# Matmul, bias and tanh on one core: twelve loads of the third column's leaving pair moved from GpSimd's DMA queue to SyncE's

## The chip, the cores and the metric

The kernel runs on one core of a Trainium2 chip. The core has a TensorE (PE in the profile; PEld is its weight load), a VectorE (DVE), a ScalarE (ACT), a GpSimd (POOL) and a SyncE (SP). Transfers between the chip's memory (DRAM) and the core's on-chip memory run on 16 DMA engines, and an instruction on POOL, SP or ACT issues them. The profile names two queues that matter here: q0, to which POOL's issues go ("software_dynamic"), and q1, to which SP's go ("hardware_dynamic"). The metric is device microseconds of one execution, the median of several.

## The reference

```python
m, k, n = 4096, 4096, 4096          # a: m x k, b: k x n, bias: n, all float32
return np.tanh(np.matmul(a, b) + bias)
```

## The kernel before

The output is made in four columns of 1024 (c = 0 to 3), and in each column in 16 row pairs of 256 rows. One row pair of one column is a 2 x 2 of 128 x 512 tiles, and the kernel makes it with seven products instead of eight, in the manner of Strassen and Winograd. `a` and `b` are split into quarters a11..a22 and b11..b22 (float16); the products are m2 = s2 b11, m5 = s5 b22, m3 = a11 d3, m1 = s1 d1, m4 = a22 d4, m6 = s6 e6 and m7 = s7 e7. s2, s5, s1, s6 and s7 are sums of quarters of `a`; d3 = b12 + b22, d1 = b11 - b22, d4 = b11 + b21, e6 = b11 + b12 and e7 = b21 + b22 belong to the column. Each right-hand operand is four blocks of 128 x 4 x 512 (`b11_0` to `b11_3` and so on); blocks 0 of b11 and of e6 are the two halves of a tile named `side`. A product of one row pair is 16 matmuls of 128 x 512.

From the second column on, row pairs are taken two at a time and some products are split once more in the same manner. In the third and fourth columns all seven are, in the function `four(n)`. For this the operands of m2 and m6 are cut into forms in DRAM (`form_m`), which are streamed through the on-chip places of b11 and e6; so b11 and e6 themselves are gone while this lasts. Some blocks of d3, d4, e7 and b22 are overwritten by a sum called t3, after their own contents have been put into DRAM (`away_m_t`).

The last two row pairs of a column are taken as a duo that shares operands with the next column: first both with blocks 0 and 1 of every operand (part 0), then both with blocks 2 and 3 (part 1), then the same two row pairs for the next column. They need b11, e6 and the rest whole. So the pair ahead of the duo in the third column leaves the split form: in `four` the flag `leave` is true for it alone, its products m1, m6 and m7 are done whole (`whole`, L961), and `give_back(c, step)`, called at numbered steps of `four` and, for steps from 18 on, from slots of the duo, brings the operands back. The table `BACK` says at which step which of them comes: ("b11", 2) is block 2 of b11; ("m5", "t3") is what t3 has overwritten in b22, ("m7", "t3") in e7, ("m3", "t3") in d3 and ("m4", "t3") in d4; ("b12", 0) and ("b21", 0) are raw blocks of the next column, which later sums need. A block of b11 or e6 that is not in `BACK` comes as soon as its place has been read for the last time (`let_go`). A block of b11 comes in two halves of 128 x 4 x 256 (256 KB each), one from `form_m` and one from `form_m` or `corner`; a raw block comes in one piece of 512 KB from a float16 copy (`cast`).

Instructions run in the order in which the program issues them, on each engine and each queue. What the leaving pair does on SP: it stores outputs (L493, from tiles `o`, `s`, `ds`), gives back the t3 places (L644) and fetches the quarters of `a` of the coming duo (L312, from `scratch`, 256 KB for each row pair of the duo). The output tiles `o` come from a pool of three, so a new one waits for the store of the one three back. In the leaving pair's tail DVE writes `o` for the second row pair (`take_m5(q)`), and behind that it takes m1 of the first row pair out of its bank into `s` (`take_m1(p)`); PE adds m7 of the first row pair into the same bank after that.

```python
        if leave:
            take_m5(q)
            take_m1(p)
```

Of the kernel before, what the change touches and what calls it, by code (L numbers as in the profile page):

```python
# [13 lines left out]
TB = 4  # L14
# [78 lines left out]


BACK = {
# [3 lines left out]
}  # L99

PLACE = {
# [6 lines left out]
HALF = (ds(0, NB // 2), ds(NB // 2, NB // 2))  # L108
# [14 lines left out]
def kernel(  # L123
# [7 lines left out]
    nc = tc.nc  # L131
# [218 lines left out]
    bop, raw = {}, {}  # L350
# [4 lines left out]
    def new_bop(name, blk):  # L355
        if blk == 0 and name in ("b11", "e6"):
            bop[name, blk] = side[:, :, ds(0 if name == "b11" else NB, NB)]
        else:
            bop[name, blk] = bops.tile([P, TB, NB], fp16, name=f"{name}_{blk}", tag=f"{name}_{blk}")
        return bop[name, blk]  # L360
# [3 lines left out]
    def cast_b(c, blk, h, j):  # L364
        cast[c, blk, h, j] = dram.tile([P, TB, NB], fp16, name=f"cast_{c}_{blk}_{h}_{j}")
        load_b(cast[c, blk, h, j], c, blk, h, j)

    def load_b(dst, c, blk, h, j, nt=TB):
        there = cast.get((c, blk, h, j))
        if there is not None and there is not dst:  # L370
            nc.gpsimd.dma_start(out=dst, in_=there)
            return
        off = b.offset + (2 * blk + h) * TB * QP * N + c * NCW + j * NB
        dx, dt = (1, QP) if h or blk else (TB, 1)
        for t in range(0, TB, nt):
            for q in (0, 2, 1, 3):
                src = bass.AP(
                    tensor=b.tensor, offset=off + (q * KQ + t * dt) * N,
                    ap=[[dx * N, QP], [dt * N, nt], [1, NB]],
                )  # L380
                nc.gpsimd.dma_start(out=dst[ds(q * QP, QP), ds(t, nt)], in_=src)  # L381

    def load_raw(name, c, blk):
        raw[name, blk] = wide.tile([P, TB, NB], fp16, name=name, tag="wide")
        nt = TB // 2 if c == 2 and name == "b21" else TB
        load_b(raw[name, blk], c, blk, *((0, 1) if name == "b12" else (1, 0)), nt)

    def load_op(name, c, blk):
        load_b(new_bop(name, blk), c, blk, *((0, 0) if name == "b11" else (1, 1)))
# [244 lines left out]
    def move(what, c, out_, *names):  # L634

        for name, (r, j) in (OVER_FOUR if c in FOURS else OVER).items():
            if names and name not in names:
                continue
            if out_:
                away[what, c, name] = dram.tile([P, TP, NB // 2], fp16, name=f"away_{what}_{c}_{name}")  # L640
            for i in range(2):
                there = away[what, c, name][:, ds(i * TB, TB)]
                here = quarter(what, r, j, i)
                nc.sync.dma_start(*(there, here) if out_ else (here, there))  # L644
# [94 lines left out]
    forms, blocks, queue, pulled = {}, {}, [], [0]  # L739
# [70 lines left out]
        corners[name, blk] = dram.tile([P, TB, NB // 2], fp16, name=f"corner_{name}_{blk}")  # L810
        nc.gpsimd.dma_start(out=corners[name, blk], in_=bop[name, blk][:, :, HALF[1]])

    def bring_block(c, name, blk):
        if (c, name, blk) not in blocks:
            what = {"b11": "m2", "e6": "m6"}[name]
            r, i = divmod(blk, 2)
            to = new_bop(name, blk)
            for j in range(2):
                there = corners[name, blk] if (r, j) == (0, 1) else forms[what, (r, j)][:, ds(i * TB, TB)]
                nc.gpsimd.dma_start(out=to[:, :, HALF[j]], in_=there)  # L820
            return
        nc.gpsimd.dma_start(out=new_bop(name, blk), in_=blocks[c, name, blk])

# [11 lines left out]
    def let_go(what, name):  # L835
        tag = held.pop((what, name))
        if returned and not queue and tag != "sum":
            name, blk = tag[:-2], int(tag[-1])
            if (name, blk) not in BACK:
                bring_block(returned[0], name, blk)  # L840
        else:
            free.append(tag)
        pull_four()
# [141 lines left out]
    def give_back(c, step):  # L985
        for (name, part), at in BACK.items():
            if at == step:
                if name in ("m3", "m4", "m5", "m7"):
                    move(name, c, False, part)
                elif name in ("b12", "b21"):  # L990
                    load_raw(name, c + 1, part)
                else:
                    bring_block(c, name, part)

    left_over = []

    def four(n):
# [11 lines left out]
        def step(k):  # L1009
            if leave:  # L1010
                give_back(c, k)
# [152 lines left out]
        if leave:  # L1164
# [27 lines left out]
            for k in range(18, 29):  # L1192
                at_slot(SLOTS * m + k - 18, give_back, c, k)
# [293 lines left out]
    def change(c, part, n):  # L1487


        s0 = SLOTS * n  # L1490
        blks = (2 * part, 2 * part + 1)
        for i, blk in enumerate(blks):
            at_slot(s0 + 1, load_op, "b11", c, blk)
            at_slot(s0 + 3, load_op, "b22", c, blk)
            at_slot(s0 + (4 if part else -3), load_raw, "b12", c, blk)
            at_slot(s0 + (8 if part else -2), load_raw, "b21", c, blk)
            s1 = s0 + 2 * part + i
            at_slot(s1 + 8, bsum, "d3", blk)
            at_slot(s1 + 9, bsum, "e6", blk)
            at_slot(s1 + 11, bsum, "d1", blk)  # L1500
            at_slot(s1 + 12, bsum, "d4", blk)
            at_slot(s1 + 13, bsum, "e7", blk)
# [87 lines left out]
    def load_first(m, queue, out_):  # L1590
# [9 lines left out]
        out=ident, in_=ident, compare_op=mybir.AluOpType.is_equal, fill=0.0,  # L1600
# [146 lines left out]
    for c in TWICE:  # L1747
# [24 lines left out]
        if c in STREAMED:  # L1772
            later = 8
            for at, name in zip((15, 15, 15, 16, 17, 19, 20), STREAM):
                at_slot(s0 + at, put_form, c, name)
            for blk in range(4):
                at_slot(s0 + 21, put_block, c, "e6", blk)
                at_slot(SLOTS * streams[c][-1] + 15, bring_block, c, "e6", blk)
            at_slot(s0 + 30, begin, c)
# [60 lines left out]
    for slot in range(1 - len(ORDER), SLOTS * len(items)):  # L1840
        if slot in handed:
            if slot - 1 not in handed:
                c = max(c for c in FOURS if SLOTS * (begins[c] - 2) < slot)
# [50 lines left out]
```

## Time and profile before

| | |
|---|---|
| median of 3 runs | 1524.16 us (1523.2 to 1524.38) |
| profiled execution | 1524.36 us, span 1522.6 us |
| TensorE busy | 1507.8 us, 99% of the span |
| DVE, ACT, POOL busy | 78%, 25%, 33% |
| q0 (POOL) / q1 (SP) | 203.22 MB / 185.24 MB |

The profiled execution lies 0.2 us above the median, and 1.8 us of it lie outside the span. The leaving pair of the third column stands at about 1060 to 1114 us from the span's start, the duo's part 0 in the third column at about 1114 to 1138 (its m6 and m7 end a little later, among products of part 1). The rows of the profile that matter for the change stand in the prediction. In the views of the profile, a row's "x" is a count; in the view of a DMA queue in a window the columns are packets, MB, and the time of its packets as a share of 16 engines.

### The profile page before, as it was taken

Reading aid. Unit: us, or ns where it says so; the run is one execution under the profiler, and the core shown is the slowest. Engines: PE = TensorE matmul, PEld = TensorE weight load, DVE = VectorE, ACT = ScalarE, POOL = GpSimd, SP = SyncE. Lnnn points to the kernel's source line nnn. Section 1 sums busy time; section 2 is a strip of 40 time slices with the busy share of each in tenths; the row PEclk is TensorE's granted clock in tenths of the full one; section 3 lists DMA queues with packets and bytes.
Section 4 is the critical chain, followed back from the end, with each engine's and each line's share of the span. In section 5 each row is a group of like instructions: output and inputs, shape, how many; then the busy total and the mean of one; then the engine's idle time right before and its main releaser. Section 6 shows DMA issues by size and latency. Waiting matters only on the chain.

```text
span 1522.6 us, 24007 instructions
## 1 busy us (share of the span) xinstructions
PE 1507.8 (99%) x9101; PEld 890.3 (58%) x9101; DVE 1182.2 (78%) x1644; ACT 380.1 (25%) x830; POOL 497.0 (33%) x893
## 2 busy tenths in 40 slices
PE   9999999999999999999999999999799999999999
PEld 4444444444445666544444578888544458888887
DVE  6789877777876666677787788888648869888888
ACT  4431111111221122111122223333113222333332
POOL 8775443333513231333543311111313121111112
PEclk9999999999999999999999999999899999999999
DMA  9999999999979998999998978889876687888895
GB/s 186 186 209 254 267 254 213 216 213 236 188 219 298 255 286 262 233 254 232 238 189 253 291 279 306 305 322 334 280 257 211 217 259 267 314 306 312 319 342 191
DMA packets 207672, 390.39 MB, mean 256 GB/s; under 512 B 25538, under 2 KB 103874, under 8 KB 207556
## 3 DMA queue, kind: packets, MB, share of 16 engines
q0 software_dynamic: 119616, 203.22, 57.5%
q1 hardware_dynamic: 87268, 185.24, 34.9%
q8 instruction: 71, 1.16, 0.3%
q10 hardware_dynamic: 672, 0.39, 0.1%
q14 instruction: 45, 0.37, 0.1%
HBM read 337.65 MB, written 136.84 MB: 312 GB/s over the span
## 4 chain that ended last, share of the span: by engine, by line
PE 97%; DMA 2%; DVE 0%; POOL 0%; ACT 0%; issue 0%; POOLq 0%; ACTq 0%; DVEq 0%
PE ps L478 55%; PE ps L897 27%; PE ps L1523 5%; PE ps L961 5%; PE ps L678 4%; DMA out_dram<-o 2%; DMA side<-in_b_dram 0%; DVE ps L153 0%; POOL first L1592 0%; POOL side L1612 0%; DVE a L153 0%; DVE ds L153 0%; ACT o L502 0%; DVE h L153 0%; DVE s L153 0%
## 5 line engine op out<-in xcount | busy, mean ns | idle before, releaser
L478 PEld LDWEIGHTS <-a 128*128 128x128 f16 x3136 | 306.9, 98 | 364.5 <-issue 0.4
L478 PE MATMUL ps<-b,a 128*128 128x512 f16 x1092 | 249.2, 379 | 0.0
L897 PEld LDWEIGHTS <-h 128*128 128x128 f16 x2176 | 212.7, 98 | 27.0 <-DVE h L153 0.8
L833 POOL DMA_DIRECT2D form<-form_m x147 | 77.7, 529 | 412.3 <-PE ps L897 370.0
L478 PE MATMUL ps<-d,a 128*128 128x512 f16 x896 | 202.5, 379 | 0.0
L478 PE MATMUL ps<-e,a 128*128 128x512 f16 x876 | 199.4, 379 | 0.0
L278 DVE STREAM_TRANSPOSE a<-nat 128x1024 f16<-128x1024 f16 (+2 forms) x202 | 175.2, 911 | 19.1 <-PE ps L478 17.6
L897 PEld LDWEIGHTS <-a 128*128 128x128 f16 x1632 | 159.6, 98 | 25.3 <-issue 0.9
L478 PE MATMUL ps<-d,s 128*128 128x512 f16 x624 | 141.0, 379 | 0.0
L250 POOL DMA_DIRECT2D nat<-in_a_dram x176 | 92.9, 533 | 133.8 <-DVE a L278 67.2
L478 PEld LDWEIGHTS <-s 128*128 128x128 f16 x816 | 79.8, 98 | 94.1
L381 POOL DMA_DIRECT2D b<-in_b_dram x192 | 103.4, 545 | 82.1 <-DVE a L278 31.0
L153 DVE TENSOR_TENSOR a<-a,a 128x2048 f16<-128x2048 f16 (+1 forms) x103 | 123.7, 1201 | 0.2
L897 PE MATMUL ps<-form,h 128*128 128x256 f16 x848 | 108.1, 273 | 0.0
L153 DVE TENSOR_TENSOR h<-a,h 128x1024 f16<-128x1024 f16 x136 | 92.4, 686 | 12.8 <-PE ps L897 12.7
L502 ACT ACTIVATE o<-ps 128x512 f32<-128x512 f32 x88 | 52.9, 601 | 153.0 <-issue 101.8
L897 PE MATMUL ps<-form,a 128*128 128x256 f16 x672 | 83.7, 273 | 0.1
L961 PE MATMUL ps<-d,a 128*128 128x512 f16 x352 | 79.4, 379 | 0.0
L153 DVE TENSOR_TENSOR ds<-ds,ps 128x512 f32<-128x512 f32 (+1 forms) x101 | 66.8, 672 | 12.6 <-PE ps L961 7.0
L983 ACT CAST ps<-zeros 128x256 f32<-128x256 f16 x140 | 50.1, 380 | 96.2 <-DVE s L153 51.3
L961 PEld LDWEIGHTS <-a 128*128 128x128 f16 x416 | 41.1, 99 | 55.0 <-issue 11.6
L153 DVE TENSOR_TENSOR ps<-ps,x 128x256 f32<-128x256 f32 x88 | 37.8, 429 | 41.8 <-PE ps L897 26.6
(198 smaller groups left out, 1967.4 us busy)
## 6 DMA issues: line engine op xcount, KB each, us to landing
form<-form_m POOLq DMA_DIRECT2D x147, 512.0 KB, 7.0
a<-scratch SPq DMA_DIRECT2D x140, 512.0 KB, 7.2
out_dram<-o SPq DMA_DIRECT2D x199, 256.0 KB, 5.7
nat<-in_a_dram POOLq DMA_DIRECT2D x288, 128.0 KB, 6.4
scratch<-a SPq DMA_DIRECT2D x48, 512.0 KB, 6.5
b<-in_b_dram POOLq DMA_DIRECT2D x160, 128.0 KB, 5.4
scratch<-a SPq DMA_DIRECT2D x32, 256.0 KB, 6.2
cast<-in_b_dram POOLq DMA_DIRECT2D x64, 128.0 KB, 9.6
```

The costliest lines, as they stand in the source:

```text
L153: nc.vector.tensor_tensor(out=out_, in0=in0, in1=in1, op=op)
L250: nc.gpsimd.dma_start(out=tl[ds(q * QP, QP), :, :], in_=src.rearrange("(mb p) k -> p mb k", p=QP),)
L278: nc.vector.transpose(dst[:, ds(b0 * tb, n * tb), :].rearrange("P (b t) (mb p) -> P mb b t p", t=tb, p=QP), src[:, :, ds(b0, n), :].rearra ...
L381: nc.gpsimd.dma_start(out=dst[ds(q * QP, QP), ds(t, nt)], in_=src)
L478: nc.tensor.matmul(st[where], at, bt, start=(what == "m2" or n < LEAD and what == "m1") and i == 0, stop=i == len(ts_) - 1, skip_group_che ...
L502: nc.scalar.activation(o, src, TANH)
L678: nc.tensor.matmul(to, at, bt, start=False, stop=t == TP - 1, skip_group_check=True)
L833: nc.gpsimd.dma_start(out=rights[what, name], in_=forms[what, name])
L897: nc.tensor.matmul(to, at, bt, start=False, stop=t == TP - 1, skip_group_check=True)
L961: nc.tensor.matmul(to[:, half], at[:, t // TB, t % TB], bop[right, t // TB][:, t % TB, half], start=anew and t == 0, stop=t == T - 1, skip ...
L983: nc.scalar.copy(bank(n, 0, where)[:, HALF[half]], zeros)
L1523: nc.tensor.matmul(mb[m % 4, j], aq[m, kt // T][:, kt % T, :], right(kt, j), start=fresh and kt == k0, stop=stop and kt == k1 - 1, skip_gr ...
```

## The change

Three things change. `BACK` is a new table: blocks 0 and 1 of b11 now come at steps 9 and 10 (before, block 0 at step 9, and block 1 as soon as its place was free), blocks 2 and 3 at step 17 (before 10 and 11), b22's t3 places at step 11 (before 10), those of d4 and d3 at 15 and 16 (before 17 and 16), the next column's b12 blocks at 18 (before 17), its b21 blocks at 19 as before. `load_raw`, `load_b` and `bring_block` take a queue, and `give_back` hands them SP's for the b12 and b21 blocks, and for every b11 or e6 block from step 8 on; that is b11 alone, since e6 blocks 0 and 1 are at 6 and 7 and blocks 2 and 3 come through `let_go`. PE, DVE and ACT execute the same instructions in the same order as before.

```diff
 BACK = {
-    ("m4", "t3"): 17, ("m3", "t3"): 16, ("m7", "t3"): 8,
-    ("b12", 0): 17, ("b12", 1): 17, ("b21", 0): 19, ("b21", 1): 19,
-    ("b11", 0): 9, ("e6", 0): 6, ("e6", 1): 7, ("m5", "t3"): 10, ("b11", 2): 10, ("b11", 3): 11,
+    ("e6", 0): 6, ("e6", 1): 7, ("m7", "t3"): 8, ("m5", "t3"): 11, ("b11", 0): 9, ("b11", 1): 10,
+    ("m3", "t3"): 16, ("b11", 2): 17, ("b11", 3): 17, ("m4", "t3"): 15,
+    ("b12", 0): 18, ("b12", 1): 18, ("b21", 0): 19, ("b21", 1): 19,
 }
+DIRECT = 8
...
-    def load_b(dst, c, blk, h, j, nt=TB):
+    def load_b(dst, c, blk, h, j, nt=TB, queue=nc.gpsimd):
...
-            nc.gpsimd.dma_start(out=dst, in_=there)
+            queue.dma_start(out=dst, in_=there)
...
-    def load_raw(name, c, blk):
+    def load_raw(name, c, blk, queue=nc.gpsimd):
...
-    def bring_block(c, name, blk):
+    def bring_block(c, name, blk, queue=nc.gpsimd):
...
-                nc.gpsimd.dma_start(out=to[:, :, HALF[j]], in_=there)
+                queue.dma_start(out=to[:, :, HALF[j]], in_=there)
...
                 elif name in ("b12", "b21"):
-                    load_raw(name, c + 1, part)
+                    load_raw(name, c + 1, part, nc.sync)
                 else:
-                    bring_block(c, name, part)
+                    bring_block(c, name, part, nc.gpsimd if step < DIRECT else nc.sync)
```

On SP, from the return of e7's t3 places (`e_0`, `e_1`) to the fourth store of the stage, there stood before (`b_0`, `b_1` are b22's places, `out_dram<-o` the stores):

```order
L644 DMA e_0_6535<-away_m_2_t_6891 128x4x256
L644 DMA e_1_6567<-away_m_2_t_6891 128x4x256
L493 DMA out_dram<-o 128x512 x3
L644 DMA b_0_6261<-away_m_2_t_6569 128x4x256
L644 DMA b_1_6266<-away_m_2_t_6569 128x4x256
L493 DMA out_dram<-o 128x512
```

and now, with line numbers one higher (`side` is b11 block 0, `b_1_9925` is block 1):

```order
L645 DMA e_0_6535<-away_m_2_t_6891 128x4x256
L645 DMA e_1_6567<-away_m_2_t_6891 128x4x256
L821 DMA side<-form_m_0_6764 128x4x256
L821 DMA side<-corner_b_0_6889 128x4x256
L494 DMA out_dram<-o 128x512 x3
L821 DMA b_1_9925<-form_m_0_6764 128x4x256
L821 DMA b_1_9925<-corner_b_1_6927 128x4x256
L494 DMA out_dram<-o 128x512
```

Two halves of a b11 block stand ahead of the three stores now and two behind them.

Further along on SP, at the end of the leaving pair, there stood before, between its last stores and the next column's bias (`d_0_6513`, `d_1_6537` are d4's places; `a_10069`, `a_10072` and `a_10128` are a21, a11 and a12 of the duo's part 1):

```order
L493 DMA out_dram<-ds 128x512
L644 DMA d_0_6513<-away_m_2_t_6856 128x4x256
L644 DMA d_1_6537<-away_m_2_t_6856 128x4x256
L312 DMA a_10069<-scratch_107 128x1024
L312 DMA a_10069<-scratch_106 128x1024
L312 DMA a_10072<-scratch_107 128x1024
L312 DMA a_10072<-scratch_106 128x1024
L312 DMA a_10128<-scratch_107 128x1024
L312 DMA a_10128<-scratch_106 128x1024
L405 DMA bias_bc<-in_bias_dram 128x512 x2
```

and now, from the second half of b11's block 2 on (`a_10065` and `a_10068` are a21 and a11, `a_10128` is a12 still; the four `b` from `cast` are the next column's b12 and b21):

```order
L821 DMA b_2_10059<-form_m_5_6886 128x4x256
L821 DMA b_3_10062<-form_m_2_6827 128x4x256
L821 DMA b_3_10062<-form_m_5_6886 128x4x256
L313 DMA a_10065<-scratch_107 128x1024
L313 DMA a_10065<-scratch_106 128x1024
L313 DMA a_10068<-scratch_107 128x1024
L313 DMA a_10068<-scratch_106 128x1024
L372 DMA b_10071<-cast_0_0_1_3504 128x2048
L372 DMA b_10073<-cast_1_0_1_3585 128x2048
L372 DMA b_10100<-cast_0_1_0_3874 128x2048
L372 DMA b_10102<-cast_1_1_0_3988 128x2048
L313 DMA a_10128<-scratch_107 128x1024
```

Four halves of b11 now stand ahead of a21 of part 1, and four blocks of 512 KB ahead of its a12. POOL's queue lost twelve rows: the eight halves of b11 and the four raw blocks; behind e6's eight halves it now has the next column's b11 and b22 at once.

More of the change, by code (lines that the diff above doesn't have):

```diff
@@ L381, in load_b @@
                 nc.gpsimd.dma_start(out=dst[ds(q * QP, QP), ds(t, nt)], in_=src)
-    def load_raw(name, c, blk):
+    def load_raw(name, c, blk, queue=nc.gpsimd):
         raw[name, blk] = wide.tile([P, TB, NB], fp16, name=name, tag="wide")
         nt = TB // 2 if c == 2 and name == "b21" else TB
-        load_b(raw[name, blk], c, blk, *((0, 1) if name == "b12" else (1, 0)), nt)
+        load_b(raw[name, blk], c, blk, *((0, 1) if name == "b12" else (1, 0)), nt, queue)
     def load_op(name, c, blk):
```

## The prediction

> **What bounds the kernel now.** I read the page first, then the waits of TensorE, the chain that ended last, the timeline around the one long wait, and then the DMA queues in short windows.
>
> ```profile
> PE 1507.8 (99%) x9101; PEld 890.3 (58%) x9101; DVE 1182.2 (78%) x1644; ACT 380.1 (25%) x830; POOL 497.0 (33%) x893
> ...
> PE ps L961 <- DVE s L153: 8.8, 1, 8.8
> PE warm L1583 <- DVE idle L416: 1.3, 1, 1.3
> ```
>
> TensorE is busy for 99% of the span, and of its waits (columns: total us, times, longest) one is long: 8.8 us at L961, the whole products of the leaving pair. The next is 1.3 us at the start. The change can therefore win this one wait and what hangs on it, or open new ones. The chain (start us, us, what) tells what it waited for:
>
> ```profile
> 1082.41 17.66 DMA out_dram<-o
> 1100.07 0.02 issue
> 1100.09 0.04 DVE o L153
> 1100.13 0.57 issue
> 1100.70 0.69 DVE s L153
> 1101.38 0.04 issue
> 1101.43 12.26 PE ps L961 x48
> 1113.68 100.15 PE ps L478 x464
> ...
> 1369.03 3.45 PE ps L961 x16
> ```
>
> The first of three stores needed 17.66 us to land. DVE's `take_m5(q)` needed its tile, `take_m1(p)` stood behind that on DVE, and TensorE restarted 1.36 us after the landing (1101.43 less 1100.07). The 48 matmuls behind it took 12.26 us, where 16 such take 3.45, so 10.35 at full speed. The timeline gives when TensorE was ready, and windows give the granted clock:
>
> ```profile
> 1089.84 2.75 PE L961 MATMUL ps<-e,a 128*128 128x512 f16 x12
> ...
> 1092.60:1101.40 8.80, 0.00 (x0) 0.10 (x1) 1.31 (x3) 0.54 (x1) 0.00 (x0) 0.62 0.88 315
> 1101.40:1105.20 3.80, 3.77 (x10) 1.42 (x10) 1.17 (x2) 0.72 (x2) 0.00 (x0) 0.53 0.71 212
> 1105.20:1113.50 8.30, 8.30 (x40) 3.69 (x39) 1.37 (x2) 1.26 (x2) 0.00 (x0) 1.00 0.87 285
> ```
>
> TensorE had ended at 1092.59, waited to 1101.43, and then had a clock of 0.53 for 3.8 us (third last column) before it was at 1.00 again. The stall costs 8.84 of waiting and 1.9 of slow clock, 10.7 us together; that is the most this stage can give.
>
> Why a store of 256 KB takes 17.66 us is in the queues (packets, MB, share; then issues with the us to landing):
>
> ```profile
> q0 software_dynamic: 585, 1.91, 66.3%
> q1 hardware_dynamic: 620, 1.05, 35.3%
> ...
> e<-away_m_t SPq DMA_DIRECT2D x2, 256.0 KB, 18.5
> e<-form_m POOLq DMA_DIRECT2D x1, 256.0 KB, 9.7
> ...
> q0 software_dynamic: 153, 0.50, 86.2%
> q1 hardware_dynamic: 157, 0.09, 20.4%
> ```
>
> The first four rows are of the window 1078 to 1087.4, the last two of 1088 to 1090. While both queues have work, they get packets one for one (585 to 620, 153 to 157), whatever a packet holds. POOL's packets are large; SP's hold 2 KB in fetches and stores, and 512 bytes in the returns from `away`, which are 128 x 4 x 256 like a half of b11. So SP's queue gets about a sixth of the bytes between 1088 and 1090, and the store, behind four fetches and two such returns, waits until POOL is done.
>
> **The change part by part.** Twelve issues leave POOL; a half block costs it 0.75 us of issuing (the four in the next row take 3.00). POOL idles 67% of the span, so that wins nothing. Twelve go onto SP, which issues little else. PE, DVE and ACT run the same order, so all else is when data land.
>
> *First step: the first store.* POOL's queue now ends with e6.
>
> ```profile
> 1075.46 3.00 POOL L820 DMA_DIRECT2D e<-form_m  x4
> ```
>
> Its last half is issued 0.78 us before the end of that row, at 1077.7, and lands 9.7 us on, at 1087.4. From then SP is alone. Until then it has moved 1.05 MB, the four fetches ahead. Left ahead of the store are two returns as before, now also two halves of b11, 1.0 MB in small packets. What SP's queue alone moves is in two windows, 1110 to 1112 (mostly 512-byte packets) and 1104 to 1110 (2 KB packets), and what 4 KB packets alone do in 1072 to 1078:
>
> ```profile
> q1 hardware_dynamic: 793, 0.50, 91.5%
> ...
> q1 hardware_dynamic: 935, 1.71, 82.9%
> ...
> q0 software_dynamic: 502, 1.75, 94.5%
> ```
>
> That is 0.25, 0.285 and 0.29 MB a us. 1.0 MB at 0.25 is 4.0 us, the store 0.9 us, so it lands at 1092.3; half a us for what was unfinished of the fetches makes 1092.8. TensorE restarts 1.36 later, at 1094.2, and waits 1.6 us instead of 8.84. The bounds: no wait, if the small packets go a little faster; and a landing at 1096.4 (a wait of 5.2), if the fourth fetch still ends as late as now, at 1091.5 (the row of two fetches below, 12.4 us after 1077.9 on the mean, 1 us more for the later). I take the near end, since that lateness is the sharing with b11, which is gone.
>
> ```profile
> a<-scratch SPq DMA_DIRECT2D x2, 256.0 KB, 12.4
> ```
>
> A wait of 1.6 us leaves the clock up (the window of 8.8 us has a mean of 0.62; between 1.00 and 0.5 that is a fall some 2.1 us into it). The next 48 matmuls take 10.35, and the duo begins at 1104.5 instead of 1113.7: a gain of 9.1 us.
>
> *Second step: what is late next.* The duo's part 1 reads its a12 in m5. SP's fetch of a12 stood directly behind those of a21 and a11; now 2 MB of b12 and b21 stand between, and 1 MB of b11 ahead of all three. In the trace:
>
> ```profile
> 1116.64 3.80 SPq L312 DMA_DIRECT2D a<-scratch  x6
> DMA to landing us min/median/max: 12.8/13.5/14.1
> ...
> 1137.69 3.62 PE L478 MATMUL ps<-b,a 128*128 128x512 f16 x16
> ```
>
> The six fetches are a21, a11 and a12; the second row is of the last two (a12), issued at 1118.6 and 1119.2, which landed at 1131.4 and 1133.4, 4 us ahead of m5 at 1137.69. That m5 comes 24.0 us after the duo's start, so at 1128.5 in the new time. What SP's queue must move from 1087.4 up to and with a12, counted from the new order in pieces of 256 KB: 16 in 512-byte packets (4.0 MB: e7's, b22's, d4's and d3's places, b11), 20 stores and fetches (5.0 MB), and four raw blocks (2.0 MB). At the rates above that is 16.0 + 17.5 + 6.9 = 40.4 us; the 0.285 was of a queue 83% busy, and with 0.34 it is 37.4. POOL meanwhile brings four blocks of the next column (2 MB), from about 6 us after the duo's start. Both together move, in 1122 to 1130:
>
> ```profile
> q0 software_dynamic: 583, 2.13, 66.7%
> q1 hardware_dynamic: 590, 1.07, 35.8%
> ```
>
> POOL's 2 MB take 7.5 us at 0.266, in which SP moves 1.0 MB instead of 2.1: 3.9 us lost. Where b11's small packets meet them, SP moves 0.045 MB a us (1088 to 1090) and loses 6.6. In sum a12 is in at 1087.4 + 41.3 to 47.0, which is 1128.7 to 1134.4, middle 1131.6. TensorE needs its first half first and the second 1.7 us later, and the first half lands 0.9 us ahead, so m5 begins at about 1130.7: a new wait of 2.2 us, between none and 5. The smaller needs on the way hold by the same count: d3's places land near 1110, m3 begins at 1111.4; b11's blocks 2 and 3 and a21 at about 1119 to 1122, m2 of part 1 begins at 1121.8. These have 1 us of room or less, and what they cost is taken from the wait at m5, which is behind them.
>
> *Clock after the second wait.* By the row of 0.62 a wait of 2.2 us may just bring the slow clock, at most its 1.9 us; I take half, 0.9.
> [...]
>
> *Sum.* 9.1 - 2.2 - 0.9 = 6.0 us. Against the profiled execution 1524.36 that is 1518.4; the median lies 0.2 lower, so **1518.2 us**. The rest of the fourth column follows unchanged, only earlier.
>
> **The rivals.** *No second wait.* If SP's queue does 0.34 MB a us on large packets and meets POOL with few small ones, a12 is in time: 9.1 us gained, 1515.1; with no first wait either, 1513.5. For it: the lower ends above. Against it: a margin of nothing.
>
> *The wait moves to part 1 and is longer* (slower). Place: m5 of part 1, behind b12 and b21 on SP, or m3 or m2 before it. It decides once a12 lands after 1137.7, that is once SP's 11 MB take over 50.3 us, less than 0.22 MB a us on the mean, sharing included. At 0.19 they need 57.9 us, a12 lands at 1145.3, and with the slow clock the kernel takes 7.6 + 1.9 = 9.5 us more: 1533.7; at 0.21 (52.4 us, 1139.8) it is 1528.3. For it: the window 1088 to 1090 above, and eight halves that went in large packets go in small ones now. Against it: both rates of SP alone are higher.
>
> *The change doesn't do what it says.* The store still lands late, since 0.5 MB has been put ahead of it on its own queue: at 1096.4 and with a part of the second wait the gain falls to 2 us or less, 1522 to 1524. For it: a queue alone that drained its last small packets slowly. Against it: POOL's 3 MB of b11 and b12 are gone from beside it.
> [...]
>
> **How the numbers follow.** A measurement of this kernel can tell 0.2% (3 us) from no change. The forecast has 0.48, nearly all of it faster; no second wait 0.16; little or nothing moved 0.18; slower by the moved wait 0.18. So faster 0.64, same 0.18, slower 0.18. The likeliest case has its own range of 1515 to 1521. The whole range goes from 1513.5, where neither wait is left, to 1526, which leaves about a tenth above and less below.
>
> **What the profile after would show.** The wait of L961 for DVE falls from 8.8 to under 3 us, and the first store lands in some 10 us instead of 17.7; POOL's queue is empty from about 1087 to 1110. TensorE has a wait that is not there now, at L479, for a fetch of `a`, of 1 to 5 us, near 1129. If the wait of L961 stays over 5 us, the first step is wrong; if the new wait is over 9 or stands at m3 or m2, the second is. A wait of DVE for b12 or b22 in the duo would be something I have not counted.

## The result, and the profile after

The median went from 1523.93 us to 1516.26 us (executions of 1514.7 to 1517.84). The ratio of the two is 0.995, with a 95% interval of 0.9935 to 0.9964, so the change is worth 5 to 10 us. The forecast was 1518.2. The profiled execution of the changed kernel took 1514.7 us, with a span of 1513.0; it is its quickest, so the profiles lie 9.7 us apart where the medians lie 7.7. The lines of the code have one number more than before: L962 is the old L961, L479 the old L478, L154 the old L153.

The row of the engines and TensorE's waits after the change (columns: total us, times, longest):

```profile
PE 1505.8 (100%) x9101; PEld 889.8 (59%) x9101; DVE 1182.5 (78%) x1644; ACT 380.3 (25%) x830; POOL 488.9 (32%) x881
...
PE warm L1584 <- DVE idle L417: 1.3, 1, 1.3
PE ps L479 <- DVE s L154: 0.9, 1, 0.9
PE ps L962 <- DVE s L154: 0.4, 1, 0.4
```

The 8.8 us at the leaving pair are down to 0.4. A wait of 0.9 at L479 is new, and it isn't for a fetch of `a`, as forecast, but for DVE. The chain that ended last (start us, us, what) tells both stories:

```profile
1082.69 8.20 DMA out_dram<-o
1090.91 0.04 DVE o L154
...
1091.52 0.69 DVE s L154
...
1092.25 3.38 PE ps L962 x15
...
1101.51 6.52 DMA out_dram<-s
...
1108.12 0.70 DVE s L154
...
1108.87 95.16 PE ps L479 x440
```

The first store now lands 8.20 us after its issue instead of 17.66, and TensorE goes on at 1092.25 instead of 1101.43. Then a later store, that of an `s`, is issued at 1101.51 and needs 6.52 us. It stands behind the four returned places of d4 and d3 on SyncE's queue. DVE wants to write that `s` again before it has landed, at 1108.03, and the first m5 of the duo, between its two row pairs, waits for DVE until 1108.87.

The window that was the long wait, as window rows have it (the third last column is the granted clock), the queues between 1088 and 1090 (packets, MB, share), and what POOL issues next in the timeline:

```profile
1092.60:1101.40 8.80, 8.80 (x43) 3.99 (x41) 2.17 (x4) 1.89 (x3) 0.00 (x0) 1.00 0.87 288
...
q1 hardware_dynamic: 477, 0.65, 109.0%
...
1105.66 0.75 POOL L372 DMA_DIRECT2D side<-cast  x1 [27.97 <-DMA d<-away_m_t]
```

TensorE is busy throughout with a granted clock of 1.00; before, it stood still in this window, with a mean clock of 0.62. SyncE's queue moves 0.65 MB in these 2 us instead of 0.09, and POOL's has no row at all: its last half of e6 landed at 1085.55, and it issues nothing for 28 us.

Where the 9.7 us between the profiles come from: the leaving pair's first part ended 0.8 us earlier already (1091.81 against 1092.59). That has nothing to do with the change: POOL's first fetch of e6, ahead of everything that moved, was already issued at 1071.70 instead of 1072.48. The wait is 8.4 shorter. The 48 matmuls after it take 10.36 us (1092.25 to 1102.61, granted clock 1.00) instead of 12.26, which saves 1.7 to 1.9. The new wait takes 0.9 back, 1.1 with the matmuls around it, and 0.2 are lost later.

The second place that the forecast watched is the fetch of a12 for part 1 of the duo. SyncE's timeline, then the time from issue to landing of those two fetches (least, median, most), then TensorE's row of m5:

```profile
1117.20 2.25 SPq L313 DMA_DIRECT2D a<-scratch  x2
DMA to landing us min/median/max: 8.1/8.8/9.4
...
1127.89 3.62 PE L479 MATMUL ps<-b,a 128*128 128x512 f16 x16
```

They were issued at 1117.20 and 1119.13 and landed at 1126.59 and 1127.26. m5 began at 1127.89 and waited for nothing: 1.3 us of room for the first half, and 2.4 for the second, which is needed 1.7 later.

### The profile page after: what moved, and what is told of

Its sections match the earlier page's. It is cut to its first block, busy times and chain, and to the rows that moved or that the text cites. A ratio compares the mean times of both kernels' runs of the same rounds, so it can differ in the third digit from the quotient of the medians.

```text
span 1513.0 us, 24012 instructions
## 1 busy us (share of the span) xinstructions
PE 1505.8 (100%) x9101; PEld 889.8 (59%) x9101; DVE 1182.5 (78%) x1644; ACT 380.3 (25%) x830; POOL 488.9 (32%) x881
## 4 chain that ended last, share of the span: by engine, by line
PE 96%; DMA 2%; DVE 1%; issue 0%; SPq 0%; ACT 0%; DVEq 0%
PE ps L479 55%; PE ps L898 27%; PE ps L1524 5%; PE ps L962 5%; PE ps L679 4%; DMA out_dram<-o 1%; DMA out_dram<-s 0%; DMA a<-scratch 0%; DMA coarse<-in_a_dram 0%; DVE ps L154 0%; PE warm L1584 0%; DVE h L154 0%; PE spread L442 0%; DVE s L154 0%; DVE d L154 0%
## 5 line engine op out<-in xcount | busy, mean ns | idle before, releaser
L479 PEld LDWEIGHTS <-a 128*128 128x128 f16 x3136 | 306.8, 98 | 365.7 <-issue 1.2
L479 PE MATMUL ps<-b,a 128*128 128x512 f16 x1092 | 249.4, 379 | 0.9 <-DVE s L154 0.9
L479 PE MATMUL ps<-d,a 128*128 128x512 f16 x896 | 202.5, 379 | 0.0
L479 PE MATMUL ps<-e,a 128*128 128x512 f16 x876 | 199.3, 379 | 0.0
L898 PEld LDWEIGHTS <-a 128*128 128x128 f16 x1632 | 159.7, 98 | 25.1 <-issue 0.7
L479 PE MATMUL ps<-d,s 128*128 128x512 f16 x624 | 141.0, 379 | 0.0
L479 PEld LDWEIGHTS <-s 128*128 128x128 f16 x816 | 79.9, 98 | 94.1
L154 DVE TENSOR_TENSOR a<-a,a 128x2048 f16<-128x2048 f16 (+1 forms) x103 | 123.9, 1203 | 0.2
L154 DVE TENSOR_TENSOR h<-a,h 128x1024 f16<-128x1024 f16 x136 | 92.6, 687 | 12.3 <-PE ps L898 12.1
L962 PE MATMUL ps<-d,a 128*128 128x512 f16 x352 | 79.4, 379 | 0.0
L154 DVE TENSOR_TENSOR ds<-ds,ps 128x512 f32<-128x512 f32 (+1 forms) x101 | 66.9, 673 | 10.8 <-PE ps L962 5.3
L154 DVE TENSOR_TENSOR ps<-ps,x 128x256 f32<-128x256 f32 x88 | 37.9, 430 | 41.5 <-PE ps L898 26.6
L479 PE MATMUL ps<-side,a 128*128 128x512 f16 x272 | 69.8, 379 | 0.0
```

Of the source, the lines that this page charges most:

```text
L154: nc.vector.tensor_tensor(out=out_, in0=in0, in1=in1, op=op)
L479: nc.tensor.matmul(st[where], at, bt, start=(what == "m2" or n < LEAD and what == "m1") and i == 0, stop=i == len(ts_) - 1, skip_group_che ...
L898: nc.tensor.matmul(to, at, bt, start=False, stop=t == TP - 1, skip_group_check=True)
L962: nc.tensor.matmul(to[:, half], at[:, t // TB, t % TB], bop[right, t // TB][:, t % TB, half], start=anew and t == 0, stop=t == T - 1, skip ...
```

## The experiments

In every one of them the theory is that of the prediction: POOL's large packets, while they are under way, leave SyncE's queue a small share (0.09 MB beside POOL's 0.50 in 1088 to 1090 before the change), and this made the first store late; a12 is the next thing that can be late.

### The changed kernel again

No edit; it is to show what the spread of the times is made of.

> The changed kernel as it is, to see what its times spread over and which wait a slower execution has. Theory (the first store decides, and the fetch a12 is just in time): 1514.5 to 1518; the profile has the first store landed within 10 us of its issue and TensorE's wait at L962 under 1 us, and where the execution is over 1516.5, a wait at m5 of the duo's part 1 (L479, for a12) of 1 to 3 us that the faster profile had not. Rival (the spread comes from the store): the slower execution has TensorE's wait at L962 at 2 us or more and none at a12.

Median 1515.74 us (1514.73 to 1516.28), ratio 0.9944 (0.9932 to 0.9957). The profiled execution took 1515.37. Its waits of TensorE:

```profile
PE ps L479 <- DVE s L154: 1.2, 1, 1.2
PE ps L962 <- DVE s L154: 0.8, 1, 0.8
```

It is 0.67 us longer than the execution profiled first, and its two waits are together 0.65 us longer (1.24 and 0.77 against 0.92 and 0.44). a12 landed at 1127.73 and 1128.41, ahead of m5 at 1128.66. So the two executions differ by the two waits for stores, and not by a12. That fits the rival in kind, though the wait at L962 was smaller than the 2 us set for it. No execution over 1516.5 was profiled, so what the one of 1517.84 waited for stays open.

### The new table, all on POOL's queue

```diff
-                    load_raw(name, c + 1, part, nc.sync)
+                    load_raw(name, c + 1, part)
...
-                    bring_block(c, name, part, nc.gpsimd if step < DIRECT else nc.sync)
+                    bring_block(c, name, part)
```

> The new table of steps, with all twelve transfers still on POOL's queue. Theory (the queue decides, by what lies beside the store): POOL still moves b11 and b12 while the store is under way, so the store needs 16 to 19 us, TensorE waits 8 to 10 us at L962, and the time is 1522.5 to 1526. Rival (the steps decide: b11's blocks 2 and 3 and b12 come later, and POOL's queue would be emptier at the store): the store lands within 12 us, the wait is under 4 us, and the time is 1515 to 1519.

1524.05 us, ratio 1.0 (0.9991 to 1.0009): nothing is left of the gain. TensorE's wait, the store in the chain, and the queues of 1088 to 1090:

```profile
PE ps L962 <- DVE s L154: 7.9, 1, 7.9
...
1081.86 16.68 DMA out_dram<-o
...
q0 software_dynamic: 150, 0.49, 85.4%
q1 hardware_dynamic: 157, 0.08, 18.1%
```

The queues get packets one for one again, 150 to 157, and SyncE's queue a seventh of the bytes. The later steps in the table hold nothing back: b12 is issued on POOL at 1088.25, as soon as its tiles are free, against 1089.02 with the old table.

### The old table, with the new queues

```diff
 BACK = {
-    ("e6", 0): 6, ("e6", 1): 7, ("m7", "t3"): 8, ("m5", "t3"): 11, ("b11", 0): 9, ("b11", 1): 10,
-    ("m3", "t3"): 16, ("b11", 2): 17, ("b11", 3): 17, ("m4", "t3"): 15,
-    ("b12", 0): 18, ("b12", 1): 18, ("b21", 0): 19, ("b21", 1): 19,
+    ("m4", "t3"): 17, ("m3", "t3"): 16, ("m7", "t3"): 8,
+    ("b12", 0): 17, ("b12", 1): 17, ("b21", 0): 19, ("b21", 1): 19,
+    ("b11", 0): 9, ("e6", 0): 6, ("e6", 1): 7, ("m5", "t3"): 10, ("b11", 2): 10, ("b11", 3): 11,
 }
```

> The old table of steps, with b11's blocks 0, 2 and 3 and b12 and b21 on SyncE's queue (block 1 of b11 is brought on POOL's, behind e6, as before). Theory (the queue decides): POOL's queue holds only 0.5 MB of b11 behind e6, the first store lands some 10 to 12 us after its issue, TensorE's wait at L962 is under 3 us; b11's blocks 2 and 3 now lie ahead of the fourth store and of s, so the wait at the duo's first m5 (0.9 in the changed kernel) grows to 1 to 5 us: 1515 to 1520. Rival (the new steps are what matters): within 3 us of the kernel before, 1521 to 1527.

1515.56 us, ratio 0.9945 (0.9931 to 0.9959): the whole gain. Its wait, and two rows of the chain:

```profile
PE ps L962 <- DVE s L154: 1.9, 1, 1.9
...
1085.38 7.28 DMA out_dram<-o
...
1094.01 10.52 PE ps L962 x48
```

With the one before, this settles which half of the change works: the queue does, the steps don't. The expected wait at the duo's first m5 did not come, for two reasons. d4's places are at step 17 in this table, behind the store of `s`, and it landed 5.8 us after its issue, at 1108.27. And TensorE, which had waited longer at L962, came to that m5 1.8 us later than in the changed kernel; there a landing at 1108.03 was too late. What is won there is lost at L962, where the 0.5 MB of b11 that POOL still moves behind e6 cost 1.2 to 1.5 us.

### b12 and b21 back on POOL, b11 on SyncE

```diff
-                    load_raw(name, c + 1, part, nc.sync)
+                    load_raw(name, c + 1, part)
```

> The changed kernel with b12 and b21 of the next column back on POOL's queue; b11 stays on SyncE's. POOL has nothing else to move then, so b12 (1 MB) goes as soon as its tiles are free, before the first store has landed. Theory (packets of the two queues go one for one, so any large packets of POOL's that are under way hold the store up, for about as long as POOL needs for them): the store lands 3 to 5 us later than in the changed kernel, TensorE waits 3 to 6 us at L962, 1518 to 1521.5. Rival (only b11 was in the way): the store lands by 1092, the wait is under 1.5 us, and the time is 1515 to 1517.

1520.18 us, ratio 0.9977 (0.9968 to 0.9987). Waits, chain, and the window behind the wait with its granted clock:

```profile
PE ps L962 <- DVE s L154: 3.3, 1, 3.3
...
PE ps L479 <- DMA a<-scratch: 0.8, 1, 0.8
...
1086.59 7.58 DMA out_dram<-o
...
1095.54 12.22 PE ps L962 x48
...
1095.50:1099.40 3.90, 3.87 (x12) 1.49 (x12) 1.18 (x2) 0.73 (x2) 0.00 (x0) 0.66 0.78 207
```

One MB of POOL's, b12, is enough for 3.3 us of waiting and a slow clock behind it (12.22 us for the 48 matmuls instead of the 10.52 above). The rival, that only b11 was in the way, falls. With b21 on POOL beside b11 and a21 on SyncE's queue, a fetch of `a` is late too, by 0.8 us.

### b11 back on POOL, b12 and b21 on SyncE

```diff
-                    bring_block(c, name, part, nc.gpsimd if step < DIRECT else nc.sync)
+                    bring_block(c, name, part)
```

> The changed kernel with b11 back on POOL's queue; b12 and b21 stay on SyncE's. Theory (as above; POOL's 2 MB of b11 are in by about 1095, and the store can't be much earlier): the store lands at 1095 to 1098, TensorE waits 4.5 to 8 us at L962, 1519.5 to 1524. Rival (SyncE's queue is short enough without b11, and the store gets through): the wait is under 2 us, 1515 to 1517.5.

1521.51 us, ratio 0.9983 (0.9974 to 0.9992).

```profile
PE ps L962 <- DVE s L154: 5.4, 1, 5.4
...
1081.76 14.24 DMA out_dram<-o
```

These rows (the wait, and the store in the chain) and those above give a series by what POOL moves behind its last half of e6 (landings by the record of each transfer):

| Kernel | MB behind e6 on POOL | last landing on POOL's queue | first store lands | wait at L962 (old L961) | median us |
|---|---|---|---|---|---|
| changed kernel, again | 0 | (e6) 1086 | 1091.3 | 0.8 | 1515.7 |
| old table, new queues | 0.5 | 1088.6 | 1092.7 | 1.9 | 1515.6 |
| b12, b21 on POOL | 1 | 1089.5 | 1094.2 | 3.3 | 1520.2 |
| b11 on POOL | 2 | 1094.7 | 1096.0 | 5.4 | 1521.5 |
| new table, all on POOL | 3 | 1097.7 | 1098.5 | 7.9 | 1524.1 |
| before | 3 | 1098.9 | 1100.1 | 8.8 | 1524.0 |

In the last three rows the store lands 0.8 to 1.3 us after POOL's queue is empty. In the first three, 0.5 MB of b11 stand ahead of the store on SyncE's queue, and it lands 4.0 to 5.2 us after that. So in all six the store comes in only when POOL's queue is empty and what stands ahead of it on its own queue has gone, and b12 on POOL delays it as b11 does.

### The kernel before, with a tile of its own for the output that waited

This leaves the queues as they were and takes away the need for the first store: the output of the leaving pair's m5 goes into a new tile.

```diff
-            st[i]["o"] = new_out()
+            st[i]["o"] = wide.tile([P, 2, NB], fp32, name="own", tag="wide")[:, 0] if leave and i == q else new_out()
```

> The kernel before, with one tile more: the output of the leaving pair's m5 goes into a tile of its own, so that DVE needn't wait for the first store. Theory (SyncE's queue as a whole was late, the store being only the first to be missed): the landing of e7's returned place t3 in the same queue is missed next, some 2 to 3 us before the old restart; TensorE still waits 5.5 to 8 us in the leaving pair, and the time is 1521 to 1523.5. Rival (only the store's tile was missing): the wait is under 1.5 us and the time 1513.5 to 1517.

1520.56 us, ratio 0.9979 (0.997 to 0.9989). The waits and the chain:

```profile
PE ps L961 <- DMA e<-away_m_t: 4.7, 2, 3.9
...
1079.89 19.61 DMA e<-away_m_t
1099.54 11.13 PE ps L961 x44
```

The theory is right in kind and off in size: TensorE is now held by e7's returned place in the same queue, which needed 19.61 us, but by 4.7 us and not 5.5 to 8, and the time lies a little under the expected 1521 to 1523.5. A buffer more takes away one of several late transfers and wins 3.5 of the 8 us; the queue had to be freed for the rest.

### b12 and b21 behind a12

```diff
-    ("b12", 0): 18, ("b12", 1): 18, ("b21", 0): 19, ("b21", 1): 19,
+    ("b12", 0): 23, ("b12", 1): 23, ("b21", 0): 24, ("b21", 1): 24,
```

> The changed kernel with b12 and b21 (2 MB on SyncE's queue) issued behind the fetches of a12 instead of ahead of them. This takes away what the prediction's second step named as the cause of a new wait at m5 of the duo's part 1. Theory (the fetch is in time by about 1 us without that): a12's halves land 4 to 7 us earlier, before 1123, and the time stays within 0.8 us of the changed kernel's, 1515 to 1516.7. Rival (in many executions the fetch is late, and that makes the changed kernel's spread): 1513.8 to 1515, with a smaller spread. Against both: if b12 now comes too late for DVE, TensorE waits in the duo and the time is over 1517.

1515.84 us (1514.77 to 1516.29), ratio 0.9944 (0.993 to 0.9957), the changed kernel's time. Its waits, then the landings of three fetches issued at 1110.7 to 1111.8, of which the last two are a12's:

```profile
PE ps L479 <- DVE s L154: 2.1, 2, 1.7
...
PE ps L962 <- DVE s L154: 0.5, 1, 0.5
...
DMA to landing us min/median/max: 11.2/11.3/11.3
```

a12 is in at 1122.4 and 1123.1, 4 to 5 us earlier, and nothing is won, because nothing was waited for there. What the forecast's second step named as a cause is at work (2 MB ahead of a12 cost it 4 to 5 us), but with it a12 still came in time. The wait for the store of `s` was 1.7 us here, although up to that store nothing differs from the changed kernel: its size changes from one execution to the next.

### d4's returned places behind the stores

Three kernels try the wait that was not forecast. The first moves only d4's two places, to step 17 behind the stores `s` and `ds` and ahead of b11's blocks 2 and 3:

```diff
-    ("m3", "t3"): 16, ("b11", 2): 17, ("b11", 3): 17, ("m4", "t3"): 15,
+    ("m3", "t3"): 16, ("m4", "t3"): 17, ("b11", 2): 17, ("b11", 3): 17,
```

> The changed kernel with one edit: d4's two returned places go behind the stores s and ds, and ahead of b11's blocks 2 and 3, on SyncE's queue; b12 and b21 stay ahead of a12. Theory (the store s is late only by d4's place ahead of it, and a12 is in time by about 1 us): the wait at the duo's first m5 is gone, m5 of part 1 comes about 1 us earlier, and so a12, which lands no earlier, is now waited for by 0 to 1 us at L479: 1514.5 to 1516, within 0.8 us of the changed kernel. If the theory has the margin at a12 wrong, nothing is waited for there and the time is 1514.2 to 1515.

1517.23 us (1516.9 to 1518.62), ratio 0.9959 (0.9946 to 0.9971): the wait for the store is gone, as expected, and a larger one is there, so the time is 1 to 1.5 us over the changed kernel's and over the expected range. The wait, and the chain up to it:

```profile
PE ps L479 <- DMA a<-scratch: 1.5, 1, 1.5
...
1114.54 7.41 DMA a<-scratch
1121.96 9.89 DMA a<-scratch
1131.90 74.42 PE ps L479 x344
```

The wait is for the two halves of a12, issued at 1121.34 and 1121.96 and landed at 1129.90 and 1131.86. That is the second wait of the forecast at its very place, m5 of part 1. SyncE issued a21 ahead of it 4 and 6 us later than in the changed kernel (1110.89 and 1114.54 against 1106.93 and 1108.32); by SyncE's own waits 3.6 us of that were for TensorE. b12, b21 and a12 stand behind that.

The second kernel puts d4 behind b11's blocks 2 and 3, and b12 and b21 behind a12:

```diff
-    ("m3", "t3"): 16, ("b11", 2): 17, ("b11", 3): 17, ("m4", "t3"): 15,
-    ("b12", 0): 18, ("b12", 1): 18, ("b21", 0): 19, ("b21", 1): 19,
+    ("m3", "t3"): 16, ("b11", 2): 17, ("b11", 3): 17, ("m4", "t3"): 17,
+    ("b12", 0): 23, ("b12", 1): 23, ("b21", 0): 24, ("b21", 1): 24,
```

> The kernel with b12 and b21 behind a12, and besides d4's four returned places moved from ahead of the stores s and ds to behind them. Theory (the wait of 0.9 to 1.2 us at the duo's first m5, which the prediction had not, comes from the store of s standing behind d4's and d3's returns on SyncE's queue): that store lands 1.5 us or more earlier, the wait is gone, and the time is 0.7 to 1.2 us under the kernel with b12 and b21 later alone. Rival (the store is held up by its issue or by d3's returns): the wait stays over 0.6 us and the times are equal within 0.4 us. If d4 comes too late for m4, TensorE waits there instead.

1516.87 us, ratio 0.9951 (0.9939 to 0.9963), 1.0 over the kernel above with b12 and b21 later alone, where 0.7 to 1.2 under it were expected. d4 has two returned places and not four; the other two are d3's, and they stayed ahead. The store lands at 1107.10 instead of 1109.32, 5.1 us after its issue instead of 7.0, and its wait is gone. So the two places of d4 ahead of it were the cause; now d4 itself is late:

```profile
PE ps L479 <- DMA d<-away_m_t: 2.0, 1, 2.0
...
1108.14 11.61 DMA d<-away_m_t
```

The third has d4 ahead of b11's blocks 2 and 3, and b12 and b21 behind a12:

```diff
-    ("m3", "t3"): 16, ("b11", 2): 17, ("b11", 3): 17, ("m4", "t3"): 15,
-    ("b12", 0): 18, ("b12", 1): 18, ("b21", 0): 19, ("b21", 1): 19,
+    ("m3", "t3"): 16, ("m4", "t3"): 17, ("b11", 2): 17, ("b11", 3): 17,
+    ("b12", 0): 23, ("b12", 1): 23, ("b21", 0): 24, ("b21", 1): 24,
```

> The same move of d4's places, with b12 and b21 behind a12 as well. Theory: neither wait is left; the store s lands near 1107, d4 lands by 1114, ahead of m4 at about 1117, and a12 by 1124: 1514 to 1515.2, 0.7 to 1.7 us under the kernel with b12 and b21 later alone. Rival (b11's blocks 2 and 3, now behind d4, are late for m2 or m7 of part 1): a new wait at L479 of 0.5 us or more near 1121, and 1515 to 1517.

1515.09 us (1513.95 to 1515.6), ratio 0.9942 (0.993 to 0.9955). The time lies in both expected ranges. A wait of 1.1 us is where the rival put it, at L479 and near 1121, but for a21, which stands behind b11's blocks, and not for b11:

```profile
PE ps L479 <- DMA a<-scratch: 1.1, 1, 1.1
...
1112.97 8.43 DMA a<-scratch
```

The last kernel adds the tile of its own to this one (the diff is that shown above):

> The kernel before this one, with the tile of its own for the output of the leaving pair's m5, so that DVE doesn't wait for the first store either. Theory (in the changed kernel e7's returned place lands by 1088, so the store is all that TensorE's last wait of 0.4 to 0.8 us at L962 stands for): the wait at L962 is under 0.2 us, and the time 0.3 to 0.8 us less than without the tile, 1513.5 to 1514.8. Rival (the s of this stage or a psum is missing next): the wait stays at 0.3 us or more.

1515.07 us (1514.34 to 1516.52), ratio 0.9945 (0.9931 to 0.9959). The wait at L962 is gone altogether, as the theory has it, but the median is no lower than without the tile and over the expected 1514.8; a wait of 0.6 us for a21 is left. These last two are 0.6 to 1.2 us under the changed kernel, while its own executions lie 3 us apart; no version here is clearly quicker. Each wait taken away in this stage uncovered another, of 0.6 to 2 us.

## Why the prediction was right, and where it wasn't

**What bounds the kernel.** Right. The long wait was the one thing to win, and the shares of the queues made it: a series of five settings of POOL's queue moved it from 0.8 to 7.9 us.
Between 1088 and 1090, with both queues at work, POOL's had 153 packets and SyncE's 157 before, and 150 and 157 with the new table on POOL. One for one holds there, but not everywhere: in 1092 to 1094 before they had 145 and 199, and in 1110 to 1112 after the change 166 and 221. The total rate between 1088 and 1090 was 294 GB/s before and 326 after, a tenth more, while SyncE's part of it went from 0.09 to 0.65 MB. With the queues alone changed, 1524.0 became 1515.6.

**First step: the store.** Right in kind, and a little too dear. From the landing of e6's last half to that of the store the forecast had 5.4 us, and it took 5.3 (1085.55 to 1090.89). It came 1.9 us earlier than forecast since e6 did: 0.8 of that is the whole program's, and 1.1 is e6's own: that half needed 8.65 us from issue to landing instead of 9.71. In all the other profiles it needed 8.4 to 9.7, so this part is within what executions differ by. So TensorE waited 0.4 and 0.8 us in two executions instead of 1.6. In the second, which lies nearer the median, the duo began 10.5 us earlier; 0.7 of that was there before the stage, so the step was worth 9.8 and not 9.1.

**Second step: the wait for a12.** This is the step that failed, by its size: 2.2 us were forecast, and it was 0 in both profiles of the changed kernel. The place and the transfer were the right ones, as the move of d4 shows, where this wait came with 1.5 us. What was off is the time that SyncE's queue needs up to a12. Its rows, in order: the queues of 1085.6 to 1127.2; SyncE's queue alone in 1098 to 1102 and in 1120 to 1126; both queues in 1110 to 1112.

```profile
q1 hardware_dynamic: 11516, 11.71, 86.7%
q0 software_dynamic: 631, 2.32, 14.6%
...
q1 hardware_dynamic: 922, 1.44, 101.6%
...
q1 hardware_dynamic: 869, 2.40, 102.9%
...
q0 software_dynamic: 166, 0.61, 82.6%
q1 hardware_dynamic: 221, 0.11, 19.6%
```

The forecast gave 41.3 to 47.0 us for this and took the middle. From e6's landing to a12's it was 41.7. That is the near end, but by two errors that cancel. The sum took a piece of 256 KB for 0.25 MB, while its rates count it as 0.26: its 44 pieces are 11.5 MB and not 11.0, as the 11.71 of the first row agree, and by its own rates it should have said some 43 to 49 us. Against that, SyncE's queue alone was quicker than forecast: 0.36 MB a us in 1098 to 1102 and 0.40 in 1120 to 1126, where the next column's b12 and b21 went, against rates of 0.285 to 0.34 and of 0.29. The price of meeting POOL's large packets was paid: in 1110 to 1112 SyncE's queue moved 0.11 MB, with b11's blocks 2 and 3 under way, and 0.49 in the 2 us before. In 1109.6 to 1118.8, where both queues were at work, SyncE's moved 1.40 MB; in the rest of the stretch it moved 0.32 MB a us. As an estimate, 11.71 MB take 37 us at that rate, which leaves about 5 for the meeting, the middle of the forecast's 3.9 to 6.6. So the rates of the queue alone were the term that was mis-sized. With 41.7 us in place of the middle, the start 1.9 us earlier and m5 itself 0.6 earlier than forecast, a wait of 2.2 us became a margin of 1.3.

**What it hadn't.** The wait at the duo's first m5 for the store of `s`, 0.9 and 1.2 us (with its consequences, 1.1 and 1.4 of the timeline), was left out; it was 1.7 us in the kernel with b12 and b21 behind a12. d3 and d4 were counted as volume ahead of a12, and d3's own need was checked, but not what stands between them and a store behind them whose tile DVE writes next. It took about half of what the second step was to take, and so the sum came out near: 9.8 less 1.4 is 8.4, where 6.0 were forecast; the medians lie 7.7 to 8.3 apart. That the forecast lies only about 2 us off is thus in part luck: a wait too many and a wait too few.

**Clock after the second wait.** The 0.9 us for it were not needed, since no wait of 2 us was left. A wait of 1.9 us cost no clock (10.52 us for the 48 matmuls, with the old table), and one of 3.3 cost 1.7 (12.22). What 2.2 us would have cost can't be told from that: as the last section shows, the clock didn't fall at a fixed time after TensorE had stopped, so a fall 2.1 us into one wait is no rule.

**The rivals.** "No second wait" (1515.1) is what happened at a12, and its time is nearer than the forecast's own. "The wait moves to part 1 and is longer" didn't happen, though the mechanism is real: 0.5 MB later in the queue brought 1.5 us of it. "The change doesn't do what it says" fell with the store's landing. Of the signs named ahead, three came (the wait at L962 under 3 us, the store in about 10 us, POOL's queue empty from 1086 to 1106) and one didn't (a new wait for `a` near 1129).

## What to carry to other kernels

Where one queue carries large packets and another small ones, look at packets and bytes of short windows: here the one with the small packets got a seventh of the bytes (0.08 of 0.57 MB in 1088 to 1090, new table on POOL), and much on it was late, of which the profile names only the first thing missed: before, the first store (17.66 us to landing), and with a tile of its own for the output, e7's place (19.61). Moving the large transfers onto the same queue put them into an order that the program sets: in the changed kernel's profile the 464 transfers of SyncE's whose landing it gives landed in the order of their issue, and the first store needed 8.20 us. Then go through that order for every store whose tile is written again soon, as for every fetch. When a sum has a margin near zero, its rates decide: take them from windows in which the queue is full (those of the forecast had it at 83% and 91%, and it moved 0.36 and 0.40 MB a us in those of 101.6% and 102.9%), and count MB in the volume as the rates do.

## What the runs showed of the hardware that was not expected

The granted clock didn't fall at a fixed time after TensorE had stopped. Window rows of the kernel before, of the one with b11 on POOL, and of the new table with all on POOL (the third last column is the granted clock) show where it fell:

```profile
1092.60:1094.73 2.13, 0.00 (x0) 0.00 (x0) 0.00 (x0) 0.00 (x0) 0.00 (x0) 1.00 1.06 354
1094.74:1101.40 6.66, 0.00 (x0) 0.10 (x1) 1.31 (x3) 0.54 (x1) 0.00 (x0) 0.50 0.83 303
...
1091.90:1097.30 5.40, 0.04 (x1) 0.10 (x1) 1.28 (x3) 0.51 (x1) 0.00 (x0) 1.00 0.76 245
1097.30:1101.20 3.90, 3.84 (x11) 1.38 (x11) 1.20 (x3) 0.75 (x2) 0.00 (x0) 0.56 0.69 183
...
1099.90:1105.57 5.67, 5.67 (x14) 2.01 (x14) 1.14 (x2) 0.70 (x2) 0.00 (x0) 0.50 0.77 193
```

Before, it fell 2.1 us after TensorE had stopped, as the forecast worked out. With b11 on POOL it was still up after 5.4 us and fell as TensorE restarted. With b12 and b21 on POOL it fell 1.2 us after the restart, an estimate from the means of 0.66 in 1095.50 to 1099.40 and 0.92 in the 4.60 us behind that. By the means of such rows it stayed at 0.50 for 3.4 us in the two kernels just named, for 6.8 in the one with a tile of its own (0.68 in 1092.60 to 1101.40, 0.82 in the 3.20 us behind that), and for 10.2 before (1094.73 to 1104.97) and in the new table with all on POOL (0.71 in 1092.00 to 1099.90, 0.50 to 1105.57). What a wait cost in clock is, as an estimate, half of the slow time that lies behind the restart: 1.7 to 1.8 us before, with b11 on POOL and with b12 and b21 on POOL (3.4 to 3.5 us slow, after waits of 8.8, 5.4 and 3.3), and 2.8 after the wait of 7.9 (5.67 us slow, in the last row). The 48 matmuls behind the restart took 12.26, 12.18 and 12.22 us, and 13.30 after the wait of 7.9, against 10.36 in the changed kernel. So the price of a wait wasn't set by its length alone.

SyncE's issues waited for its own earlier transfers. In the changed kernel the two fetches of a12 were held up (SyncE's waits, in the stretch 1095 to 1122):

```profile
SPq L313 <- DMA a<-scratch: 2.9, 2, 1.6
```

They were issued at 1117.20 and 1119.13, 0.06 and 0.02 us after the landings, at 1117.14 and 1119.11, of the transfers that were eight issues ahead of them. In the trace of the changed kernel SyncE's 531 transfers use eight semaphores in turn, 66 or 67 transfers each, and each of these two took the one whose transfer had just landed. So in this stretch the queue held no more than eight at a time, as between 1110.88 and 1113.77; whether the program sets that or the chip, no run here tells.
